# A decoder layer on one core: sums of weights ahead end with job u, u's second column half is requested earlier, the bias is turned two granules sooner

## The chip, the core and the metric

One core of a Trainium2 chip runs the whole kernel as one program. The metric is the device time in microseconds; the kernel before took 1565.01 us (median of 3 runs, 1563.86 to 1565.57). The engines named here are TensorE (PE for its matmuls, PEld for its weight loads), VectorE (DVE), ScalarE (ACT), GpSimd (POOL) and SyncE (SP). SyncE here only issues DMAs (queue q1 in the profile); GpSimd issues the other DMAs (queue q0) beside some elementwise work. Each engine works through its own queue in the order in which the program was written, and waits for the others by semaphores.

## The reference

One layer of a decoder with two mixers side by side, on 512 tokens of width 2048, float32. Cut to what matters:

```python
h = rms_norm(x, norm_g)
proj = h @ w_in                                   # 2048 x 10800
q, kv, g_logits, z_a, uv, z_b, merge_logits = split(proj)
o_a = nsa_attention(q, kv..., g_logits) * silu(z_a)
uv = gelu(uv); u, v = split(uv)                   # 1024 columns each
v = layer_norm(v, ln_v_g, ln_v_b)
o_b = u * (tril(w_s) @ v + b_s) * silu(z_b)       # per group and chunk of 128 tokens
g_a, g_b = split(sigmoid(merge_logits))
x = x + (g_a * (o_a @ w_up_a) + g_b * (o_b @ w_up_b)) @ w_out
x = x + sigmoid(x @ w_ple_gate) * (p @ w_ple)
out = rms_norm(x, final_g)
```

The bias of the title is `b_s` (`sgu_b` in the kernel), 8 groups by 128 positions; `w_s` is `sgu_w`.

## The kernel before

**Products in two parts.** A float32 product is made of three matmuls on rounded parts: each operand is split into a high part (a ScalarE cast, line 142) and a low part (the rest, a VectorE subtraction, line 148), and high x high, low x high and high x low are summed in PSUM (lines 348 to 350).

**Jobs.** All matrix products are jobs in one list, and one generator, `gemm`, issues their matmuls in order. `fill(n)` draws n pieces from it, `finish(name)` draws until a job is done; code between such calls puts its own instructions (transposes, loads, stores) into the stream at that place. The order of everything is thus written out by hand.

**Jobs of kind "S".** They compute 512 tokens by 1024 columns over 2048 rows with seven half-size products instead of eight (Strassen's scheme). The weights fall into four blocks: b11 and b12 (upper rows, first and second half of the columns) and b21 and b22 (lower rows). Products are named 1 to 7. Product 5 uses b12 - b11, 6 uses b22 - that sum, 7 uses the result less b11 (written over b11), 4 uses b21 less what stands in b12 by then. These sums of weights are made on VectorE, in place (`sum_to`, line 255).

**Granules.** A product goes over four pairs of 128-row tiles; such a pair is a granule (an entry of `subs`): 12 matmuls, four draws of `fill`. A job of kind S has 28 granules. Job u (the first half of uv) has the order 1, 2, 5, 6 and 3 in turn, 7, 4; the jobs after it (vn, zb and m0 to m3) run 1 and 5 in turn, 6 and 3, 7, and 2 and 4. Three PSUM banks hold products: 1, 6, 7 and 4 go to the first, 5 and 3 to the second, 2 to the third. So product 4 adds into the banks that product 7 filled, once the additions of line 688 have read them. Products 1, 5 and 6 are first copied out by ScalarE (line 675).

**Loads.** `add_job` lists the weight loads of a job, 512 KB each, in the order in which SyncE issues them. Each tag has a ring of tiles: raw 3 (b21 and b22 pass through it), b11 4, b12 4. `load_next` (line 231) issues loads in that order and stops at the first whose tile isn't free yet, or whose pool isn't open (b12 lives in the pool "quad", which is opened at line 1357, after the attention phase, and lies on memory that the attention's tiles had; line 1361 calls `load_next` right after). For u the order is four b11, four b21, four b12, four b22, and four b21 again (b21').

**Running ahead.** Before the matmuls of granule si, `split_to(si + 2)` issues the high and low parts for granules up to two ahead, the sums for one more, and, where `state["sums"]` is over 1, the sums up to `state["sums"]` granules further. `state["sums"]` is 4 from the end of job za7 to the end of u, and 1 otherwise. `sum_to` leaves off where a load that it needs hasn't been issued, but it doesn't ask whether the load has landed: the VectorE instruction waits for that in its queue.

**Around u.** While u runs, the program loads the bias and the spatial weights (`bn`, `wn`, lines 1366 to 1368), turns them on TensorE in between (lines 1483 to 1495: the bias after 20 draws, the two halves of `wn` after four more each) and then starts the background list: four `oa_chunk`s of 16 items that split the attention output and form its sums (lines 1379 to 1418), drawn `state["pops"]` at a time per granule during u and vn; `assert not background` stands behind vn. The second copy of product 1 (`keep1`) takes the tile that `bn` had (tag "s1", two buffers).

Of the kernel before, what the change touches and what calls it, by code (L numbers as in the profile page):

```python
# [22 lines left out]
S = 512  # L23
# [33 lines left out]
def products(job):  # L57
    return [(p, j) for pair in job.order for j in range(job.kt // 4) for p in pair]
# [6 lines left out]
def kernel(ctx: ExitStack, tc: tile.TileContext, x, p, norm_g, w_in,  # L65
# [15 lines left out]
    def bank(kind, name):  # L81
        return psum.tile([P, 512], F32, tag=kind, name=name)
# [51 lines left out]
    def flush():  # L134
        todo = list(deferred)
        deferred.clear()
        for f in todo:
            f()

    def high(hi, src, scale=None):  # L140
        if scale is None:
            nc.scalar.copy(hi, src)  # L142
        else:
            nc.scalar.mul(hi, src, scale)

    def low(hi, lo, src, scale=None):
        if scale is None:
            nc.vector.tensor_tensor(out=lo, in0=src, in1=hi.bitcast(F32), op=ALU.subtract)  # L148
        else:
            nc.vector.scalar_tensor_tensor(out=lo, in0=src, scalar=scale, in1=hi.bitcast(F32),  # L150
                                           op0=ALU.mult, op1=ALU.subtract)
# [10 lines left out]
    jobs, subs, loads = [], [], []  # L162
# [6 lines left out]
    def add_load(tag, src, n, cols):  # L169
        r = ring_loads[tag]  # L170
        before.append(r[-rings[tag]] if len(r) >= rings[tag] else None)
        r.append(len(loads))
        loads.append((tag, src, n, cols))
        last_sub.append(None)
        return len(loads) - 1

    def weights(job, k, n, c0):
        return job.w[k * P:(k + n) * P, c0:c0 + job.cols].rearrange("(k p) c -> p k c", p=P)

    def add_job(job):  # L180
        jobs.append(job)
        if job.kind == "S":
            half, c2 = job.kt // 2, job.c2
            ld = {}
            direct = job.order[0] == "1"
            for tags in ("b11", "b21", "b12", "b22", "b21'") if direct else (("b11", "b12"), ("b22",), ("b21",)):
                for j in range(half // 2):
                    for tag in (tags,) if direct else tags:
                        c, k = (job.c0, c2)[tag[2] == "2"], half * (tag[1] == "2") + 2 * j
                        ld[tag, j] = add_load(tag if tag[1] == "1" else "raw", weights(job, k, 2, c), 2, job.cols)  # L190
            for p, j in products(job):
                if not direct:
                    ld["b21'", j] = ld["b21", j]
                last = {"7": ("b11",), "4": ("b12", "b21'"), "3": ("b22",)}.get(p, ())
                if direct and p == "2":
                    last = ("b21",)
                for tag in last:
                    last_sub[ld[tag, j]] = len(subs)
                subs.append((job, p, j, ld))
            return  # L200
        first = 0
        while first < job.kt:
            n = min(job.per_load, job.kt - first)
            li = add_load("raw", weights(job, first, n, job.c0), n, job.cols)
            for k in range(first, first + n, job.per_sub):
                last_sub[li] = len(subs)
                subs.append((job, k, min(job.per_sub, first + n - k), (li, first)))
            first += n

    raw, parts = {}, {}  # L210
    state = {"loads": 0, "sum": 0, "high": 0, "low": 0, "ahead": 0, "more": 1, "pops": 2, "due": 0, "b11": 0, "sums": 1}

    def ring(i, dtype, n=2):

# [16 lines left out]
    def load_next():  # L231
        while state["loads"] < len(loads):
            b = before[state["loads"]]
            if b is not None and last_sub[b] >= state["low"]:
                return
            if loads[state["loads"]][0] != "raw" and ("free" if loads[state["loads"]][0] == "b11" else "pool") not in quad:
                return
            load_to(state["loads"])
# [3 lines left out]
    def sum_to(i):  # L242

        while state["sum"] <= min(i, len(subs) - 1):
            job, p, j, ld = subs[state["sum"]]
            if job.kind != "S" or p not in "5674":
                state["sum"] += 1
                continue
            if any(ld[tag, j] not in raw for tag in ("b11", "b12") + {"6": ("b22",), "4": ("b21'",)}.get(p, ())):
                return  # L250
            state["sum"] += 1
            b = {tag: raw[ld[tag, j]] for tag in ("b11", "b12") + {"6": ("b22",), "4": ("b21'",)}.get(p, ())}
            o, x, y = {"5": ("b12", "b12", "b11"), "6": ("b12", "b22", "b12"),
                       "7": ("b11", "b12", "b11"), "4": ("b12", "b21'", "b12")}[p]
            nc.vector.tensor_tensor(out=b[o], in0=b[x], in1=b[y], op=ALU.subtract)  # L255

    def source(i):
        job, k, n, ld = subs[i]
        if job.kind == "S":
            return raw[ld[{"1": "b11", "5": "b12", "6": "b12", "3": "b22", "7": "b11", "2": "b21", "4": "b12"}[k], n]]  # L260
        return raw[ld[0]][:, k - ld[1]:k - ld[1] + n]

    def narrow(job, p):

        return job.kind == "S" and job.order[0] == "1" == p

    def split_to(i, more=1):
        while state["high"] < len(subs):
            h = state["high"]
            job, k, n, ld = subs[h]  # L270
            if h > (i if job.kind == "S" else i + more):
                break
            sum_to(h)
            if job.kind == "S" and narrow(job, k):
                hi = [stream.tile([P, job.cols], F32R, tag="hi", name="hi", bufs=4) for _ in range(2)]
                src = source(h)
                for a in range(2):
                    high(hi[a], src[:, a])
                parts[h] = [hi, None, src]
                state["high"] += 1  # L280
                continue
            if job.kind == "S":
                hi = quad["pool"].tile([P, 2, job.cols], F32R, tag="hs", name="hs", bufs=3)
            elif k >= job.kt - job.tail:
                hi = f_tiles["tail"]("h", k - job.kt + job.tail)
            else:
                hi = stream.tile([P, n, job.cols], F32R, tag="hi", name="hi", bufs=4)
            src = source(h)
            high(hi, src)
            parts[h] = [hi, None, src]  # L290
            state["high"] += 1
        sum_to(i + 1)
        while state["low"] <= min(i, state["high"] - 1):
            job, k, n, ld = subs[state["low"]]
            pt = parts[state["low"]]
            if job.kind == "S" and narrow(job, k):
                pt[1] = [stream.tile([P, job.cols], F32R, tag="lo", name="lo") for _ in range(2)]
                for a in range(2):
                    low(pt[0][a], pt[1][a], pt[2][:, a])
                state["low"] += 1  # L300
                load_next()
                continue
            if job.kind == "S":
                pt[1] = quad["pool"].tile([P, 2, job.cols], F32R, tag="ls", name="ls", bufs=3)
            elif k >= job.kt - job.tail:
                pt[1] = f_tiles["tail"]("l", k - job.kt + job.tail)
            else:
                pt[1] = stream.tile([P, n, job.cols], F32R, tag="lo", name="lo")
            low(*pt)
            state["low"] += 1  # L310
            load_next()
        if state["sums"] > 1:
            sum_to(i + state["sums"])

    done = set()

# [101 lines left out]
    def fill(n):  # L418
        for _ in range(n):
            next(run, None)  # L420

    def finish(name):
        while name not in done:
            next(run)
        flush()
# [192 lines left out]
    for cg in range(4):  # L618
        job = Job(f"pl{cg}", "N", w_ple, 512 * cg, 512, 2, lambda k: (pl_in["h"][:, k], pl_in["l"][:, k]),
                  evac_ple(cg), (xs, ys)[cg % 2])  # L620
        if cg == 0:
            job.per_load = 1
        add_job(job)
# [409 lines left out]
    with tc.tile_pool(name="cmp", bufs=1) as cmp:  # L1033
# [47 lines left out]
        c = cmp.tile([P, 1], F32, name="hid_c")  # L1081
# [235 lines left out]
    for s in range(n + 3):  # L1317
# [4 lines left out]
        if s < n:  # L1322
            ft, j = slots[s][0], s % 6
# [139 lines left out]
    def s4_chunk(c, new_sum=new_sum):  # L1463
# [8 lines left out]
        def second():  # L1472
# [5 lines left out]
    nc.gpsimd.memset(tri, 1.0)  # L1478
    nc.gpsimd.affine_select(out=tri, in_=tri, pattern=[[1, P]], compare_op=ALU.is_ge, fill=0.0,
                            base=0, channel_multiplier=-1)  # L1480
    state["pops"] = 1.33
    state["sums"] = 4
    fill(20)
    b = bank("o", "ps_b")
    nc.tensor.transpose(b[:, :8], bn, ident[:8, :8])
    nc.vector.tensor_copy(sgu_bt, b[:, :8])
# [14 lines left out]
            for i, a in enumerate((act_h, act_l)):  # L1501
                nc.gpsimd.dma_start(a(slice(4 * q, 4 * q + 4), slice(256, 512)), s3_dram[:, i, 4 * q:4 * q + 4])

    finish("u")
    state["sums"] = 1
    finish("vn")
    assert not background

# [358 lines left out]
```

## Time and profile before

| | us |
|---|---|
| median of 3 runs | 1565.01 |
| the profiled execution, its time | 1565.86 |
| its span in the trace | 1564.2 |
| job u, first matmul to that of vn | 489.93 to 580.40 |

The profile is one execution on the chip, times in microseconds from the span's start. A row of the timeline gives start, duration, engine, line of the kernel, operation, the tile written and the tile read, their shapes, how often, and in square brackets the idle time just before it and what ended it. A row of the waits gives who waited for whom, the total, how often and the longest. A row of a window gives its length, the busy time of PE, PEld, DVE, ACT and POOL with the number of instructions, the granted TensorE clock (1.00 is full), the share of the DMA engines and GB/s. A row of DMA issues ends in the KB of each and the median time from issue to landing; a row of a DMA queue gives packets, MB and its share of the 16 engines. Weight tiles read "raw" or "b" (buffer numbers are left out, so b11 and b12 are both "b"); "hs" and "ls" are the high and low parts of a granule.

### The profile page before, as it was taken

How to read it: one execution, taken by the hardware profiler on the slowest of the kernel's cores; microseconds unless marked ns; L12 is line 12 of the kernel's file. 1: busy time of each engine (PE TensorE's matmuls, PEld its weight loads, DVE VectorE, ACT ScalarE, POOL GpSimd, SP SyncE). 2: the span in 40 equal slices, each digit the busy share in tenths (PEclk: the TensorE clock that was granted, in tenths of full speed). 3: DMA queues.
4: the chain of work that ended last, by engine and by line, in shares of the span. 5: the costliest groups of instructions: out<-in, count | busy, mean ns of one | idle time of the engine just before them, and what ended most of it. 6: DMA issues, size and time to landing. Idle time of an engine off the chain costs nothing.

```text
span 1564.2 us, 20523 instructions
## 1 busy us (share of the span) xinstructions
PE 1541.0 (99%) x7438; PEld 1289.5 (82%) x7438; DVE 1194.1 (76%) x1869; ACT 786.0 (50%) x1345; POOL 252.3 (16%) x413
## 2 busy tenths in 40 slices
PE   9999999999999989999999999999999999999997
PEld 7889988888887868888888888888888888888885
DVE  6557758888886877978887777777656587888876
ACT  6434446667665445555544444444423343544555
POOL 1201101101122232301121211220122221000000
PEclk9999999999999999999999999999999999999999
DMA  8436731213235884917473737675742387464665
GB/s 318 129 81 194 221 81 48 61 48 108 74 90 189 245 270 131 287 54 242 133 266 103 270 100 243 206 265 205 265 153 88 122 259 245 148 202 165 185 205 185
DMA packets 161429, 269.23 MB, mean 172 GB/s; under 512 B 9752, under 2 KB 80048, under 8 KB 158768
## 3 DMA queue, kind: packets, MB, share of 16 engines
q1 hardware_dynamic: 116240, 151.67, 31.1%
q0 software_dynamic: 44944, 116.00, 22.3%
q8 instruction: 58, 0.95, 0.2%
q14 instruction: 43, 0.35, 0.1%
q10 hardware_dynamic: 144, 0.26, 0.0%
HBM read 209.69 MB, written 58.20 MB: 171 GB/s over the span
## 4 chain that ended last, share of the span: by engine, by line
PE 93%; DVE 3%; DMA 1%; ACT 1%; issue 1%; DVEq 0%; POOL 0%; SPq 0%; POOLq 0%; ACTq 0%
PE ps_m L348 7%; PE ps_m L349 7%; PE ps_m L350 6%; PE ps_za L374 2%; PE ps_t L1197 2%; PE ps_za L375 2%; PE ps_za L376 2%; PE ps_ub L388 2%; PE ps_wo L386 2%; PE ps_ub L386 2%; PE ps_ub L387 2%; PE ps_wo L387 2%; PE ps_wo L388 2%; PE ps_wo L348 2%; PE ps_pg L348 2%; PE ps_ua L348 2%
## 5 line engine op out<-in xcount | busy, mean ns | idle before, releaser
L148 DVE TENSOR_TENSOR ls<-b,hs 128x1024 fp32r<-128x1024 f32 x196 | 239.7, 1224 | 118.3 <-ACT hs L142 117.3
L142 ACT CAST hs<-b 128x1024 fp32r<-128x1024 f32 x196 | 206.1, 1053 | 236.3 <-PE ps_m L350 86.3
L148 DVE TENSOR_TENSOR lo<-raw,hi 128x512 fp32r<-128x512 f32 (+1 forms) x216 | 151.5, 706 | 80.8 <-issue 24.4
L142 ACT CAST hi<-raw 128x512 fp32r<-128x512 f32 (+1 forms) x216 | 129.3, 606 | 136.2 <-PE ps_ub L388 48.5
L142 ACT CAST hs<-raw 128x1024 fp32r<-128x1024 f32 x80 | 84.1, 1054 | 94.4 <-PE ps_m L350 35.4
L148 DVE TENSOR_TENSOR ls<-raw,hs 128x1024 fp32r<-128x1024 f32 x80 | 97.8, 1222 | 14.0 <-ACT hs L142 13.9
L255 DVE TENSOR_TENSOR b<-b,b 128x1024 f32<-128x1024 f32 x80 | 97.5, 1219 | 10.1 <-DMA b<-in_w_in_dram 10.1
L255 DVE TENSOR_TENSOR b<-raw,b 128x1024 f32<-128x1024 f32 x80 | 97.5, 1219 | 5.2 <-DMA raw<-in_w_in_dram 5.2
L348 PE MATMUL ps_m<-hs,act_h 128*128 128x512 f32 x256 | 100.5, 393 | 0.0
L349 PE MATMUL ps_m<-ls,act_h 128*128 128x512 f32 x256 | 99.7, 389 | 0.0
L350 PE MATMUL ps_m<-hs,act_l 128*128 128x512 f32 x256 | 99.7, 389 | 0.0
L142 ACT CAST pth<-ps_t 128x512 fp32r<-128x512 f32 (+1 forms) x88 | 48.0, 545 | 65.6 <-PE ps_t L1197 65.3
L1158 ACT ACTIVATE prob<-prob,st 128x512 f32<-128x512 f32 (+3 forms) x128 | 70.7, 556 | 4.0 <-DVE st L1149 3.8
L148 DVE TENSOR_TENSOR ptl<-ps_t,pth 128x512 fp32r<-128x512 f32 (+1 forms) x88 | 56.3, 640 | 20.9 <-ACT pth L142 19.9
L1149 DVE CUSTOM_DVE_ANT_0 prob<-ps_s,b 128x512 f32<-128x512 f32 (+3 forms) x128 | 56.3, 486 | 9.9 <-PE ps_s L1146 9.7
L350 PEld LDWEIGHTS ps_m<-hs,act_l 128*128 128x128 f32 x256 | 48.1, 188 | 10.1
L348 PEld LDWEIGHTS ps_m<-hs,act_h 128*128 128x128 f32 x256 | 48.1, 188 | 9.8
L349 PEld LDWEIGHTS ps_m<-ls,act_h 128*128 128x128 f32 x256 | 48.1, 188 | 9.6
L374 PE MATMUL ps_za<-act_h,hi 128*128 128x512 f32 x128 | 55.7, 435 | 0.0
L374 PE MATMUL ps_q<-act_h,hi 128*128 128x512 f32 x128 | 53.6, 419 | 0.0
L1197 PEld LDWEIGHTS ps_t<-ident,prob 128*128 128x128 f32 x320 | 39.7, 140 | 13.7 <-DVE ptl L148 2.8
L1197 PE MATMUL ps_t<-ident,prob 128*128 128x128 f32 x320 | 49.5, 273 | 1.4 <-DVE ptl L148 1.3
(641 smaller groups left out, 4399.5 us busy)
## 6 DMA issues: line engine op xcount, KB each, us to landing
raw<-in_w_in_dram SPq DMA_DIRECT2D x112, 512.0 KB, 3.8
b<-in_w_in_dram SPq DMA_DIRECT2D x56, 512.0 KB, 5.7
raw<-in_w_out_dram SPq DMA_DIRECT2D x24, 512.0 KB, 4.2
raw<-in_w_ple_gate_dram SPq DMA_DIRECT2D x24, 512.0 KB, 4.1
raw<-in_w_up_b_dram SPq DMA_DIRECT2D x16, 512.0 KB, 3.7
hsum<-h_stage POOLq DMA_DIRECT2D x12, 512.0 KB, 4.3
gate<-keep POOLq DMA_DIRECT2D x24, 256.0 KB, 4.5
oa_d<-oa_g POOLq DMA_DIRECT2D x40, 128.0 KB, 3.2
```

Source lines behind the costliest of these rows:

```text
L142: nc.scalar.copy(hi, src)
L148: nc.vector.tensor_tensor(out=lo, in0=src, in1=hi.bitcast(F32), op=ALU.subtract)
L255: nc.vector.tensor_tensor(out=b[o], in0=b[x], in1=b[y], op=ALU.subtract)
L348: nc.tensor.matmul(o, ah, wh, start=st, stop=False, skip_group_check=go)
L349: nc.tensor.matmul(o, ah, wl, start=False, stop=False, skip_group_check=go)
L350: nc.tensor.matmul(o, al, wh, start=False, stop=sp, skip_group_check=go)
L374: nc.tensor.matmul(ps, hi[:, j], ah, start=st, stop=False)
L386: nc.tensor.matmul(o, ah[:, sl], hi[:, j], start=st, stop=False)
L387: nc.tensor.matmul(o, ah[:, sl], lo[:, j], start=False, stop=False)
L388: nc.tensor.matmul(o, al[:, sl], hi[:, j], start=False, stop=sp)
L1158: nc.scalar.activation(sl, sl, AF.Exp, bias=st[:, 0, j, hh:hh + 1], scale=-1.0, accum_out=st[:, 1, j, hh:hh + 1])
L1197: nc.tensor.transpose(b[:, (2 * e + hh) * P:(2 * e + hh + 1) * P], pts[hh][:, c:c + P], ident)
```

## The change

Four edits. First, in u's list of loads the fourth b21 load moves behind the four b12 loads. Second, the extra lookahead of the sums is no longer a state that is set and reset around u: in u it still reaches four granules beyond the granule being split, but not beyond u's last one. Third, the bias is turned after 12 draws instead of 20, three granules into u instead of five, and all that follows it in the program (the turns of `wn`, the start of the background) comes two granules sooner. Fourth, the background is drawn at 1.3 instead of 1.33 items a granule. The call `finish("u")` that stood only to reset the state goes with it.

```diff
@@ add_job
-            for tags in ("b11", "b21", "b12", "b22", "b21'") if direct else (("b11", "b12"), ("b22",), ("b21",)):
-                for j in range(half // 2):
-                    for tag in (tags,) if direct else tags:
-                        c, k = (job.c0, c2)[tag[2] == "2"], half * (tag[1] == "2") + 2 * j
-                        ld[tag, j] = add_load(tag if tag[1] == "1" else "raw", weights(job, k, 2, c), 2, job.cols)
+            groups = [[(tag, j) for j in range(half // 2) for tag in tags] for tags in
+                      ((("b11",), ("b21",), ("b12",), ("b22",), ("b21'",)) if direct else (("b11", "b12"), ("b22",), ("b21",)))]
+            if direct:
+                groups[2].append(groups[1].pop())
+            for group in groups:
+                for tag, j in group:
+                    c, k = (job.c0, c2)[tag[2] == "2"], half * (tag[1] == "2") + 2 * j
+                    ld[tag, j] = add_load(tag if tag[1] == "1" else "raw", weights(job, k, 2, c), 2, job.cols)
@@ split_to, at its end
-        if state["sums"] > 1:
-            sum_to(i + state["sums"])
+        job = subs[min(i, len(subs) - 1)][0]
+        if job.kind == "S" and job.order[0] == "1":
+            more = i + 1
+            while more < i + 4 and subs[more + 1][0] is job:
+                more += 1
+            sum_to(more)
@@ around u
-    state["pops"] = 1.33
-    state["sums"] = 4
-    fill(20)
+    state["pops"] = 1.3
+    fill(12)
     b = bank("o", "ps_b")
     nc.tensor.transpose(b[:, :8], bn, ident[:8, :8])
     nc.vector.tensor_copy(sgu_bt, b[:, :8])
...
-    finish("u")
-    state["sums"] = 1
     finish("vn")
```

More of the change, by code (lines that the diff above doesn't have):

```diff
@@ L210 @@
     raw, parts = {}, {}
-    state = {"loads": 0, "sum": 0, "high": 0, "low": 0, "ahead": 0, "more": 1, "pops": 2, "due": 0, "b11": 0, "sums": 1}
+    state = {"loads": 0, "sum": 0, "high": 0, "low": 0, "ahead": 0, "more": 1, "pops": 2, "due": 0, "b11": 0}
     def ring(i, dtype, n=2):
```

## Prediction

> **What bounds the kernel.** The page of the profile comes first, then the waits of TensorE alone, then the timeline of TensorE, VectorE and the DMA queues where those waits lie.
>
> ```profile
> PE 1541.0 (99%) x7438; PEld 1289.5 (82%) x7438; DVE 1194.1 (76%) x1869; ACT 786.0 (50%) x1345; POOL 252.3 (16%) x413
> ```
>
> ```profile
> PE ps_u L348 <- DVE keep L688: 6.5, 1, 6.5
> PE ps_u L349 <- DVE ls L148: 2.2, 1, 2.2
> ...
> PE ps_t L1197 <- DVE ptl L148: 1.3, 1, 1.3
> ```
>
> TensorE is busy 99% of the span, so only what keeps it waiting, or keeps its clock down, can be won. Two waits of the whole execution are over 2 us, and both lie in job u, the job that is edited. Its matmuls, in the timeline (start, duration):
>
> ```profile
> 489.93 0.39 PE L348 MATMUL ps_u<-hi,act_h 128*128 128x512 f32 x1
> 500.81 0.39 PE L348 MATMUL ps_u<-hs,act_h 128*128 128x512 f32 x1
> 503.62 0.23 PE L1485 MATMUL ps_b<-ident,bn 8*128 8x8 f32 x1
> 503.78 0.49 PE L348 MATMUL ps_u<-hs,act_h 128*128 128x512 f32 x1
> 506.44 0.58 PE L349 MATMUL ps_u<-ls,act_h 128*128 128x512 f32 x1 [2.17 <-DVE ls L148]
> 510.44 0.39 PE L350 MATMUL ps_u<-hs,act_l 128*128 128x512 f32 x1
> 560.56 0.39 PE L350 MATMUL ps_u<-hs,act_l 128*128 128x512 f32 x1
> 567.46 0.76 PE L348 MATMUL ps_u<-hs,act_h 128*128 128x512 f32 x1 [6.52 <-DVE keep L688]
> 571.98 0.40 PE L350 MATMUL ps_u<-hs,act_l 128*128 128x512 f32 x1
> 580.40 0.39 PE L348 MATMUL ps_vn<-hs,act_h 128*128 128x512 f32 x1
> ```
>
> Granules are counted from 0, so u has 0 to 27; each is 12 matmuls. The first four (48 matmuls) run from 489.93 to 500.81: 0.2267 us each, 2.72 us a granule. From 503.78 to 510.44 lie 11 matmuls, 2.49 us at that pace and 6.66 in fact: **4.17 us lost**. From 560.56 to 571.98 lie 12, 2.72 us at that pace and 11.42 in fact: **8.70 us lost**. Together 12.87. As a cross-check, u's 336 matmuls need 76.17 us of the 90.47 between its first and vn's; beside the 12.87 that leaves 1.43 for the nine small transposes in between and a few tenths.
>
> (The matmul at 560.56 is the last of product 7, granule 23.) Part of each loss is idle time, part is clock. The stretch behind the 1.3 us wait of the third line (it ends at 304.3), and the one behind the 2.2 us wait (columns: length, busy us of PE, PEld, DVE, ACT, POOL, granted clock, DMA share, GB/s):
>
> ```profile
> 305.00:308.00 3.00, 3.00 (x19) 2.60 (x19) 2.93 (x14) 2.74 (x10) 0.00 (x0) 1.00 0.00 0
> ```
>
> ```profile
> 506.44:510.20 3.76, 3.76 (x10) 2.97 (x11) 3.76 (x5) 0.01 (x1) 0.00 (x0) 0.55 0.98 335
> ```
>
> After 2.17 us of idle the clock was granted at 0.55 for 3.8 us; after 1.3 us it stayed at 1.00. So a wait of a little over a microsecond costs itself, one of 2.2 costs nearly double. Now what VectorE and the SyncE queue did:
>
> ```profile
> 497.37 1.22 DVE L148 TENSOR_TENSOR ls<-raw,hs 128x1024 fp32r<-128x1024 f32 x1
> 504.03 1.23 DVE L255 TENSOR_TENSOR b<-b,b 128x1024 f32<-128x1024 f32 x1 [5.44 <-DMA b<-in_w_in_dram]
> 505.17 1.22 DVE L148 TENSOR_TENSOR ls<-raw,hs 128x1024 fp32r<-128x1024 f32 x1
> ```
>
> and at the second place:
>
> ```profile
> 559.64 1.22 DVE L148 TENSOR_TENSOR ls<-b,hs 128x1024 fp32r<-128x1024 f32 x1
> 565.49 1.22 DVE L255 TENSOR_TENSOR b<-b,b 128x1024 f32<-128x1024 f32 x1 [4.62 <-DMA b<-in_w_in_dram]
> 566.63 1.28 DVE L688 TENSOR_TENSOR keep<-ps_u,keep 128x512 f32<-128x512 f32 x2
> ```
>
> ```profile
> 498.61 0.37 SPq L227 DMA_DIRECT2D raw<-in_w_in_dram  x1
> 499.09 2.93 SPq L227 DMA_DIRECT2D b<-in_w_in_dram  x4
> ```
>
> Both losses are one mechanism. VectorE runs in order; a sum of weights (L255), asked for ahead of need, stands in its queue before its load has landed, and urgent work stands behind it. At 498.6 the sum is product 5's first (b12 of u), and behind it is the low half of granule 5. At 560.9 it is vn's first sum, and behind it are the two L688 additions that empty the banks into which product 4 must accumulate. The loads are late for a reason, too: the four b12 requests stand in the SyncE queue behind the fourth b21 load, which may go only when VectorE has finished with the first one (498.6).
>
> **The change, part by part.**
>
> *Sums end with u.* The limit i+4 no longer crosses into vn, so vn's first sum is not queued at granule 23. Removes the wait at 560.9: 8.70 us. What is late next: the first matmul of granule 24 is due at 560.79 and needs L688 on its bank. L148 of granule 25 ends at 560.86, one L688 is 0.64 of the pair's 1.28, and 567.46 less 566.63+0.64 gives 0.19 for the signal: 561.7, 0.9 us late. With VectorE a little less behind (it then has not lost 2 us at 533 to a load, nor carried the o_a work, below) 0.4. I take **+0.6**, bounds 0 and 1.0; at that size the clock holds, by the row at 305. vn's sum now comes with the ordinary lookahead, at granule 26, two granules and 0.6 us after 560.79, i.e. 566.8. Its load:
>
> ```profile
> 558.63 6.74 DMA b<-in_w_in_dram
> ```
>
> This is the chain's piece for it: landed at 565.37, ahead of 566.8 (both by the old clock, on which they shift together); cost nothing, its cover is the three granules that the sum goes back.
>
> *b12 asked for ahead of the last b21.* The four requests are now emitted when the pool opens, right after the attention phase. That pool lies on the attention's tiles, whose last reader is the first of these lines of GpSimd; the others are the loads of its queue that follow:
>
> ```profile
> 489.02 0.73 POOL L1234 TENSOR_TENSOR o<-o,oc 128x256 f32<-128x256 f32 x1 [5.11 <-DVE o L1233]
> 489.69 0.56 POOL L1315 DMA_DIRECT2D ob_h<-hsum  x1
> 490.24 0.56 POOL L1315 DMA_DIRECT2D ob_l<-hsum  x1
> 490.77 1.55 POOL L1367 DMA_DIRECT2D wn<-in_sgu_w_dram  x2
> 492.27 0.58 POOL L1368 DMA_DIRECT2D bn<-in_sgu_b_dram  x1
> ```
>
> So b12 goes out at about 489.75 instead of 499.09, 9.3 us sooner, and the SyncE queue has nothing else to do between (its next item, the fourth b21, may not go before 498.6 anyway; it then waits behind at most the rest of b12 and is needed at granule 7, about 509.5). The first b12 took 4.9 us before; even at twice that it lands at 499.6, and the sum has until the low half of granule 5, due at 503.8 less 2.4 of VectorE work, 501.4. The 4.17 us go.
>
> *Bias two granules sooner.* The transpose of bn moves from behind granule 4 (it stands at 503.62) to behind granule 2, due at 489.93 + 36 x 0.2267 = 498.09; the two turns of wn follow a granule each. The instructions stay the same: cost nothing in themselves. They free something: the second keep copy of product 1 shares bn's buffer and waited for that transpose.
>
> ```profile
> 503.88 0.59 ACT L675 COPY keep<-ps_u 128x512 f32<-128x512 f32 x1 [2.97 <-PE ps_b L1485]
> ```
>
> Those 2.97 us of ScalarE lie under VectorE's 5.44 now; they would become the next wait were the bias left in place, and I count them at 0. But bn must have landed at 498.09. Before, its issue at 492.27 plus this row gave 497.1:
>
> ```profile
> bn<-in_sgu_b_dram POOLq DMA_DIRECT2D x1, 4.0 KB, 4.8
> ```
>
> It stands behind 1.57 MB (two of 512 KB, two of 256) in the GpSimd queue, which now shares the engines with 2.1 MB of b12. Where the two queues compete (1116 to 1120, mean 385 GB/s):
>
> ```profile
> q0 software_dynamic: 264, 1.02, 64.6%
> q1 hardware_dynamic: 263, 0.52, 36.5%
> ```
>
> The GpSimd queue keeps two thirds, about 255 KB/us. Some 1.2 MB of it fall after 493, once both are flowing: 4.7 us instead of about 3.6, so bn lands near 498.2, and with 0.2 for the signal TensorE waits **0.3**. Bounds: 0, and all of b12 ahead of bn, 2.1 MB at 385 = 5.4 us, bn at 502.5: 4.4 idle plus a slow stretch like the one above (4.17 less 2.17, 2.0), 6.4. I stay near the lower end, since the shared row is measured.
>
> The Trainium skill bears on the price of such a wait: "TensorE: Matmul & The Clock Gate", section "Why this matters for your kernels", asks for no idle gaps over about 3 us. By that rule a bias wait of 2 us would cost only itself. This trace disagrees: 2.17 us idle was followed by a granted clock of 0.55. By the rule a 2.2 us wait leaves about 10 us of gain, by the trace about 8.
>
> *Background (o_a) two granules sooner, 1.3 instead of 1.33 a granule.* The same VectorE work, two lines like the first, two like the second and one of half size, 3.4 us, over granules 14 to 18 instead of 16 to 20. VectorE is close to full there, and the third line is the tightest point:
>
> ```profile
> 543.17 0.88 DVE L431 TENSOR_TENSOR oa_f<-oa_f 128x256 f32<-128x256 f32 x2
> 549.30 0.69 DVE L150 SCALAR_TENSOR_TENSOR oa_f<-oa_f,oa_g 128x512 fp32r<-128x512 f32 x1
> ...
> 553.97 1.22 DVE L148 TENSOR_TENSOR ls<-b,hs 128x1024 fp32r<-128x1024 f32 x1
> ```
>
> It ends at 555.19; granule 22 is due at 560.79 - 5.44 = 555.35 and uses it in its second matmul, 0.4 us later. Moving o_a forward relieves that point and loads granules 14 to 17 (four low halves and four sums at 1.14 us each, the distance from 504.03 to 505.17, and o_a: 12.5 us of work in 10.9), 1.6 late against a lookahead of two granules, 5.4 us, less one cast and one low half. Cost 0; up to +1.5 if the cover fails; if anything a gain.
>
> Sum: -4.17 - 8.70 + 0.6 + 0.3 = **-12.0 us**. The profiled span of 1564.2 becomes 1552.2. That execution took 1565.86; the median of the runs is 1565.01, and I take the difference from it: **1553.0**.
>
> **Rivals.** (a) *The bias waits long.* If q0's startup suffers, bn lands around 500.3: 2.2 idle and 2.0 of clock, 3.9 more than counted: 1556.9; at the far bound 1559.1. For it: the slack is nil. Against: the two-thirds share. (b) *b12 doesn't go earlier*, because the pool's opening or a semaphore holds SyncE until about 498: the first loss stays, 12.0 - 4.17 + 0.3: 1556.9. Against: the last reader ends at 489.75, and nothing of the DMA engines' own holds it, which are idle just before (last two columns):
>
> ```profile
> 485.00:490.00 5.00, 5.00 (x28) 4.27 (x27) 1.44 (x3) 1.46 (x4) 0.98 (x2) 1.00 0.00 0
> ```
>
> (c) *The wait moves into vn, and it gets slower.* vn's four b12 loads are released by product 4's low halves. If each lands later than its sum stands in the queue and PE pays a loss like the first (4.17), four of them are 16.7: 1569.7. It decides once a load takes more than about 11 us: 6.74 now, 8.2 to the sum's place at 566.8, and from there two granules less a sum, a cast (1.05, the 2.97 us row's engine) and a low half. With two or three such losses the gain is about used up, 1561 to 1565.5. Against: vn's later sums already run with this short lookahead, and no wait of TensorE in vn is on the list. (d) *Only half a gain*: VectorE's piling up at 14 to 17 costs one wait of 2 us with clock: 1557.0.
>
> **Numbers.** Forecast 0.72 (own range 1551.5 to 1554.8: both new waits at nothing give 1565.01 - 12.87 = 1552.1, less a little for o_a's tight point; both at their likelier upper sizes, 1.0 and 1.5, give 1554.6), (a) 0.11, (b) 0.05, (c) 0.07, (d) 0.05. The range 1551.5 to 1557.2 holds the forecast, (b), (d) and half of (a). No change means within 0.2%, 3.1 us, about what a measurement tells apart. Faster 0.93, all but (c); of (c), same 0.02 where two or three of its losses come, slower 0.05 where all four do.
>
> **What would show it.** No VectorE wait on b<-in_w_in_dram in u; b12 issued by SyncE near 490; u from first matmul to vn's in 78.5 us instead of 90.5; the granted clock at 1.00 throughout u; a wait of 0.3 before ps_b and of 0.6 before product 4's first matmul. Wrong if a wait over 2 us on bn, or on b in vn, appears with a slow stretch behind it.

## The result, and the profile after

| | before | after |
|---|---|---|
| median (7 runs each, side by side), us | 1563.86 (1562.82 to 1565.57) | 1559.38 (1559.0 to 1560.73) |
| the profiled execution, its time | 1565.86 | 1559.0 |
| its span | 1564.2 | 1557.3 |
| u's first matmul to vn's | 90.47 | 82.61 |
| wo's first matmul to pg's (two of the last jobs) | 170.64 | 173.15 |

The changed kernel takes 0.9973 of the time before (95% interval 0.9961 to 0.9985): 4.5 us less, where 12.0 had been forecast. 1559.38 lies above the range of 1551.5 to 1557.2.

The page's line of engines and the waits of TensorE in the changed kernel; line numbers have moved by seven (L688 is now L695, L348 to L350 are L355 to L357).

```profile
PE 1538.7 (99%) x7438; PEld 1288.9 (83%) x7438; DVE 1195.3 (77%) x1869; ACT 785.0 (50%) x1345; POOL 252.8 (16%) x413
```

```profile
PE ps_b L1491 <- DMA bn<-in_sgu_b_dram: 2.8, 1, 2.8
PE ps_wo L394 <- DVE lo L148: 2.2, 1, 2.2
...
PE ps_u L355 <- DVE keep L695: 0.4, 1, 0.4
```

Both waits that headed the list before are gone, the 6.5 down to the hand-over of 0.4. Two others stand in their place: TensorE waits 2.8 us for the bias's load, and 2.2 us in wo, 770 us behind the place of the change (wo is the product with `w_out`, pg the one with `w_ple_gate`). TensorE's timeline around u:

```profile
489.60 0.39 PE L355 MATMUL ps_u<-hi,act_h 128*128 128x512 f32 x1
500.72 0.19 PE L1491 MATMUL ps_b<-ident,bn 8*128 8x8 f32 x1 [2.79 <-DMA bn<-in_sgu_b_dram]
502.39 0.63 PE L355 MATMUL ps_u<-hi,act_h 128*128 128x512 f32 x1
561.21 0.47 PE L355 MATMUL ps_u<-hs,act_h 128*128 128x512 f32 x1 [0.38 <-DVE keep L695]
572.21 0.39 PE L355 MATMUL ps_vn<-hs,act_h 128*128 128x512 f32 x1
```

The bias is turned at 500.72; it was due at 497.93. The matmul at 502.39 takes 0.63 instead of 0.39. The windows of the same trace (length, busy PE, PEld, DVE, ACT, POOL, granted clock, DMA share, GB/s) show why:

```profile
498.88:502.30 3.42, 1.58 (x7) 1.35 (x8) 1.87 (x4) 0.00 (x0) 0.00 (x0) 1.00 1.05 407
502.30:505.71 3.41, 3.41 (x12) 2.65 (x11) 1.09 (x1) 1.10 (x3) 0.00 (x0) 0.50 0.79 248
505.71:509.12 3.41, 3.41 (x19) 2.88 (x18) 2.96 (x3) 1.53 (x4) 1.82 (x4) 1.00 0.47 102
```

3.41 us at half clock behind the wait: 1.7 us of work lost, 4.5 with the idle time. So u is shorter by 4.17 + 8.70 - 0.38 - 4.5 = 8.0 by these terms, and by 7.86 in fact. Of the span's 6.9 us less, 7.86 come from u, 0.33 from its earlier start and 1.2 from the last part behind pg's first matmul (176.2 to 174.9; the other traces have 174.7 to 175.4); wo gives 2.51 back. The profiled execution of before took 2.0 us more than the median, that of after 0.4 less, so the medians differ by less than the spans.

The four b12 requests and the bias's load, in the timelines of SyncE's queue and of GpSimd:

```profile
489.44 2.35 SPq L230 DMA_DIRECT2D b<-in_w_in_dram  x4
```

```profile
491.94 0.58 POOL L1375 DMA_DIRECT2D bn<-in_sgu_b_dram  x1
```

And vn's first sum on VectorE, with no bracket behind it: no wait.

```profile
566.53 1.22 DVE L258 TENSOR_TENSOR b<-b,b 128x1024 f32<-128x1024 f32 x1
```

The bias's load took 8.6 us from issue to landing (4.8 before). What the queues moved up to its landing at 500.58 (packets, MB, share of the 16 engines), in 490 to 493 and in 493 to 500.6 of the changed kernel:

```profile
bn<-in_sgu_b_dram POOLq DMA_DIRECT2D x1, 4.0 KB, 8.6
```

```profile
q1 hardware_dynamic: 222, 0.45, 64.5%
q0 software_dynamic: 40, 0.16, 17.2%
```

```profile
q0 software_dynamic: 517, 1.67, 61.6%
q1 hardware_dynamic: 615, 1.17, 43.3%
```

and of the GpSimd queue in the kernel before, in 490 to 493 and in 493 to 497, when the bias landed (497.05):

```profile
q0 software_dynamic: 99, 0.41, 54.1%
```

```profile
q0 software_dynamic: 458, 1.43, 95.1%
```

Up to 493 GpSimd's queue got 0.16 MB through where it had got 0.41, although the changed kernel issues these loads 0.33 us earlier. SyncE's packets were there first: its b12 requests go out at 489.44, GpSimd's first load at 489.37, but up to 492 only SyncE's queue moves anything (0.28 MB); in the kernel before, GpSimd's had moved 0.21 MB by then. From 493 on, in the changed kernel, GpSimd's moved 1.67 MB in 7.6 us, 220 KB/us, instead of 1.43 MB in 4.05. In the rows above a packet of GpSimd's queue carries 3.2 KB (1.67 MB by 517) and one of SyncE's 1.9 KB (1.17 by 615); in the forecast's row near 1116 it was 3.9 and 2.0 KB at 264 to 263 packets. The two queues seem to share by packets rather than by bytes; that is read off these rows and was not varied.

### The profile page after: what moved, and what is told of

Same layout as the page of the kernel before. It is cut to its first block, busy times and chain, and to the rows that moved or that the text cites. A ratio compares the mean times of both kernels' runs of the same rounds, so it can differ in the third digit from the quotient of the medians.

```text
span 1557.3 us, 20518 instructions
## 1 busy us (share of the span) xinstructions
PE 1538.7 (99%) x7438; PEld 1288.9 (83%) x7438; DVE 1195.3 (77%) x1869; ACT 785.0 (50%) x1345; POOL 252.8 (16%) x413
## 4 chain that ended last, share of the span: by engine, by line
PE 94%; DVE 3%; DMA 1%; ACT 1%; issue 1%; POOL 0%; DVEq 0%; POOLq 0%; ACTq 0%
PE ps_m L355 7%; PE ps_m L357 7%; PE ps_m L356 7%; PE ps_t L1204 2%; PE ps_ub L394 2%; PE ps_ub L393 2%; PE ps_ub L395 2%; PE ps_za L381 2%; PE ps_za L382 2%; PE ps_za L383 2%; PE ps_pg L356 2%; PE ps_wo L355 2%; PE ps_pg L357 2%; PE ps_ua L356 2%; PE ps_ua L355 2%; PE ps_zb L356 2%
## 5 line engine op out<-in xcount | busy, mean ns | idle before, releaser
L355 PE MATMUL ps_m<-hs,act_h 128*128 128x512 f32 x256 | 100.5, 393 | 0.0
L357 PE MATMUL ps_m<-hs,act_l 128*128 128x512 f32 x256 | 99.6, 389 | 0.0
L357 PEld LDWEIGHTS ps_m<-hs,act_l 128*128 128x128 f32 x256 | 48.1, 188 | 10.1
L355 PEld LDWEIGHTS ps_m<-hs,act_h 128*128 128x128 f32 x256 | 48.1, 188 | 9.7
L394 PE MATMUL ps_wo<-lo,act_h 128*128 128x512 f32 x128 | 49.9, 390 | 2.2 <-DVE lo L148 2.2
```

The lines of the kernel that those rows point to most:

```text
L355: nc.tensor.matmul(o, ah, wh, start=st, stop=False, skip_group_check=go)
L357: nc.tensor.matmul(o, al, wh, start=False, stop=sp, skip_group_check=go)
L394: nc.tensor.matmul(o, ah[:, sl], lo[:, j], start=False, stop=False)
```

## The experiments

Every experiment but the last was timed in five rounds (the one with 20 draws and 1.33 items a granule has four runs) beside the kernel before, whose medians were 1564.73 (the first four), 1563.98 (the next four) and 1563.62 (the last two). Medians of different groups can thus differ by a microsecond for no reason in the kernel. The edits are those of the section on the change, first to fourth. "Length of u" is from its first matmul to vn's.

### The kernel before with the second edit alone

```diff
-        if state["sums"] > 1:
-            sum_to(i + state["sums"])
+        job = subs[min(i, len(subs) - 1)][0]
+        if job.kind == "S" and job.order[0] == "1":
+            ...
+            sum_to(more)
```

(`state["sums"]` and its call `finish("u")` go with it.)

> Before, with edit 2 alone: sums of weights end with u; the loads' order, the bias after 20 draws and 1.33 items a granule as before. Theory (the bias wait is the price of the change, all else is as forecast): the wait of VectorE on vn's first b12 goes, the one near 504 stays; u takes 90.5 - 8.3 = 82.2 us from its first matmul to vn's, the time falls by about 8. Rival (the gain is taken back behind u, where the changed kernel shows a new wait of 2.2 us in wo): u 82.2 us too, but the time falls by 5 or less.

1556.23 us (1555.85 to 1557.98), ratio 0.995 (0.9937 to 0.9962). Length of u 82.45. Its waits of TensorE:

```profile
PE ps_u L353 <- DVE ls L148: 2.9, 2, 2.5
...
PE ps_u L352 <- DVE keep L692: 0.9, 1, 0.9
```

8.0 us of u's length go: the wait of 6.5 and its slow clock were the sum of vn's in VectorE's queue, as forecast. The hand-over of 0.9 that is left is the size that the forecast worked out for a VectorE that runs behind (0.9, taken at 0.6). One thing was not expected: the first wait stayed, was longer than before (2.54 against 2.17), and the clock stayed full behind it. Windows of this trace:

```profile
501.55:504.96 3.41, 2.29 (x10) 1.42 (x8) 0.99 (x1) 1.50 (x3) 0.76 (x1) 1.00 1.05 389
504.96:508.38 3.42, 1.99 (x9) 1.64 (x10) 3.42 (x4) 1.06 (x2) 1.32 (x3) 1.00 0.92 313
508.38:511.79 3.41, 3.41 (x19) 2.83 (x18) 3.41 (x5) 1.05 (x1) 0.00 (x0) 1.00 1.07 413
```

Here the idle time (503.85 to 506.39) is divided between two windows, and neither is idle for more than 1.43 us. The last section comes back to it.

### The kernel before with the first edit alone

```diff
+            if direct:
+                groups[2].append(groups[1].pop())
```

> Before, with edit 1 alone: b12 asked for ahead of the last b21; sums still cross into vn, bias after 20 draws. Theory: bn lands near 500.5 as in the changed kernel (the queues share), but its transpose stands at 503.3, so nothing waits; the wait near 504 goes, ScalarE's second keep copy still waits for the transpose and may cost up to 0.5; the wait of 8.7 us at 560 stays. u 86.3 to 86.9 us, the time 3.6 to 4.2 below before. Rival (early b12 loads hurt more than the bias, through hsum, b22 or wn): u 88 us or more.

1559.4 us (1558.03 to 1561.03), ratio 0.9968 (0.9955 to 0.998). Length of u 86.67, 3.8 less, as expected; the median falls by 5.3 where 3.6 to 4.2 were expected, the profiled execution, the slowest of the five, by 3.7. The first wait is gone, the second stands unchanged:

```profile
PE ps_u L351 <- DVE keep L691: 6.5, 1, 6.5
```

The bias landed at 500.49, 3.4 us later than before, with the bias's turn still at its old place (503.36), where nobody waited for it. So the delay comes from the first edit, and only the third lets TensorE meet it.

### The changed kernel with the third and fourth edit undone

```diff
-    state["pops"] = 1.3
-    fill(12)
+    state["pops"] = 1.33
+    fill(20)
```

> The changed kernel with edits 3 and 4 undone: bias after 20 draws, 1.33 items a granule. Theory: no wait on bn, so the changed kernel's 2.8 us of idle and 1.7 us of slow clock go; ScalarE's keep copy waits for the transpose again, up to 0.5 us of TensorE; u 78.0 to 78.8 us against 82.6, the time 4 below the changed kernel's 1559.4, 1555 to 1556. Rival (the ScalarE wait of 3 us takes the place of the bias wait): u 80 to 82 us, 1557 to 1559. Rival (taken back behind u): u 78 us, time 1558 or more.

1552.11 us (1551.82 to 1552.4), ratio 0.992 (0.9907 to 0.9934). Length of u 78.31, and neither a wait for the bias nor one in wo; both are undone with these two edits. That is why the time is 3 us below the 1555 to 1556 expected, which left the wait in wo where it was. In u's length the two first edits add up: 8.02 and 3.80 by themselves, 12.16 together. ScalarE does wait for the bias's turn:

```profile
503.58 0.59 ACT L682 COPY keep<-ps_u 128x512 f32<-128x512 f32 x1 [2.97 <-PE ps_b L1491]
```

Nobody on the path waits for ScalarE there. The third edit frees this copy, and gains nothing by it.

### The changed kernel, bias first in GpSimd's queue

```diff
-    load_sums(slice(6, 8))
     ph_ab.close()
     ...
+    nc.gpsimd.dma_start(bn, sgu_b)
     for hf in range(2):
         nc.gpsimd.dma_start(wn[hf], ...)
-    nc.gpsimd.dma_start(bn, sgu_b)
+    load_sums(slice(6, 8))
```

> The changed kernel with the GpSimd queue reordered: bn first, then wn, then the last hsum loads (ob_h, ob_l), instead of ob_h, ob_l, wn, bn. All transfers and the bias's place (12 draws) are as in the changed kernel. Theory: bn lands before 495 beside b12's start, TensorE waits for nothing at 498; wn lands near 497, ahead of its turns; u 77.8 to 78.4 us, 1555 or a little less. Rival (the whole of DMA traffic is too much at this place, so the wait moves to wn or to b12's sums): a new TensorE wait of over 1 us between 498 and 515, u 80 us or more.

1555.7 us (1554.36 to 1557.69), ratio 0.9946 (0.9932 to 0.9959). Length of u 78.16. The bias's load and the waits over 1.5 us:

```profile
bn<-in_sgu_b_dram POOLq DMA_DIRECT2D x1, 4.0 KB, 3.6
```

```profile
PE ps_wo L394 <- DVE lo L148: 2.0, 1, 2.0
```

The same 4 KB land 3.6 us after their issue (at 493.28) when nothing stands ahead of them, with the same b12 loads beside them, and the whole loss near 498 is gone. It was the queue, not the turn of the bias. The wait in wo stays, so it has another cause.

### The wait in wo: the counter of the background

Each granule adds `state["pops"]` to `state["due"]` and draws one item for every whole unit; the rest is carried on. u, vn and zb are 84 granules: 84 x 1.33 = 111.72 leaves 0.72 in the counter, 84 x 1.3 = 109.2 leaves 0.20. Behind zb the rate is set anew, the counter is not. This kernel is the changed one with the old remainder put in:

```diff
     for g in range(8):
         background.extend(group(g))
-    state["pops"] = 1
+    state["pops"], state["due"] = 1, 0.72
```

> The changed kernel with one number put back: behind job zb the fraction of a background item that is carried on (state due) is set to 0.72, what 84 granules at 1.33 leave, instead of 0.20, what 84 at 1.3 leave. u, vn and zb are untouched. Theory (the carried fraction shifts the sums of wo by a granule, and that makes the new wait of 2.2 us near 1273): u 82.6 us as in the changed kernel, with its wait on bn; no wait of TensorE over 1 us in wo; the time 2.5 to 3.5 below the changed kernel's, 1556 to 1557. Rival (the wait in wo comes from u ending earlier, or by chance): wo keeps a wait of about 2 us, 1559 to 1560.

1554.98 us (1554.64 to 1556.22), ratio 0.9944 (0.9932 to 0.9957): 4.4 us less than the changed kernel by the medians, where 2.5 to 3.5 were expected (the part on why the prediction was wrong comes back to it). Length of u 82.68 with the bias's wait of 2.87 as before; no wait in wo, whose length is 170.62. GpSimd in wo, first in the changed kernel:

```profile
1258.34 0.72 POOL L1459 DMA_DIRECT2D s_d<-stage  x1 [2.82 <-DVE stage L148]
1259.05 0.77 POOL L1678 DMA_DIRECT2D x_d<-x  x1
1261.59 1.38 POOL L1723 DMA_DIRECT2D x2t_d<-x2t  x2 [1.76 <-DVE x2t L148]
```

then in this one:

```profile
1253.93 0.72 POOL L1459 DMA_DIRECT2D s_d<-stage  x1 [1.24 <-DVE stage L148]
1256.32 0.78 POOL L1678 DMA_DIRECT2D x_d<-x  x1 [1.67 <-DVE x L815]
1261.50 1.38 POOL L1723 DMA_DIRECT2D x2t_d<-x2t  x2 [4.40 <-DVE x2t L148]
```

At 0.7 items a granule the smaller remainder puts a background sum one granule later. Its store (s_d) comes 4.4 us later, and the store of x (x_d, 1 MB), which stands behind it in GpSimd's queue, 2.7 us. The two x2t stores (512 KB each) are issued at the same time in both kernels, but in the changed one behind an x_d that is still under way. Its row there, issue to landing:

```profile
x_d<-x POOLq DMA_DIRECT2D x1, 1024.0 KB, 7.3
```

and with the old remainder, where it has landed at 1260.9:

```profile
x_d<-x POOLq DMA_DIRECT2D x1, 1024.0 KB, 4.6
```

The landing of the x2t stores releases a tile for which ScalarE waits, in the changed kernel and then in this one:

```profile
1270.70 0.59 ACT L142 CAST x2t<-ps_x 128x512 fp32r<-128x512 f32 x1 [6.33 <-DMA x2t_d<-x2t]
```

```profile
1266.20 1.07 ACT L142 CAST x2t<-ps_x 128x512 fp32r<-128x512 f32 x2 [1.87 <-DMA x2t_d<-x2t]
```

VectorE's half of the same split waits for ScalarE (the row names its next copy, line 1698), and wo's next low part stands behind it in VectorE's queue (the changed kernel):

```profile
1272.60 1.29 DVE L148 TENSOR_TENSOR x2t<-ps_x,x2t 128x512 fp32r<-128x512 f32 x2 [5.11 <-ACT third L1698]
1273.80 0.74 DVE L438 TENSOR_TENSOR third<-ps_x,third 128x256 f32<-128x256 f32 x2
1274.46 0.68 DVE L148 TENSOR_TENSOR lo<-raw,hi 128x512 fp32r<-128x512 f32 x1
```

TensorE waits for that low part until 1275.20. All twelve traces divide the same way: where the remainder is 0.20, ScalarE waits 6.1 to 6.4 us there, where it is 0.72, 1.7 to 2.6. In kind it is the loss of before again: work that may wait stands in VectorE's queue ahead of work that may not.

The cross-check puts the new remainder into the kernel with 20 draws and 1.33 a granule, which had no wait in wo:

```diff
-    state["pops"] = 1
+    state["pops"], state["due"] = 1, 0.2
```

> The kernel with the bias after 20 draws and 1.33 items a granule (the two other edits in), with the carried fraction set to 0.20 behind zb. Theory: u as there, 78.3 us; the wait of about 2 us in wo appears, 1555 to 1556 against 1552.1 without it. Rival (by chance, or by u's length): no wait in wo, 1552.

1553.82 us (1553.54 to 1554.44), ratio 0.9935 (0.9923 to 0.9948): 1.7 us more than with 0.72, and 2.5 more when each is set against the before beside it; 1555 to 1556 had been expected. The wait comes back with nothing else changed:

```profile
PE ps_wo L394 <- DVE lo L148: 1.7, 1, 1.7
```

### The changed kernel with the first edit undone

```diff
-            if direct:
-                groups[2].append(groups[1].pop())
```

> The changed kernel with edit 1 alone undone: b12 again behind the fourth b21; sums end with u, bias after 12 draws, 1.3 items. Theory (bn is late because b12 shares the DMA engines with the GpSimd queue): bn lands near 497.0, TensorE doesn't wait for it at 498; the wait of VectorE on b12 near 504 is back, about 4 us of TensorE; u 81.5 to 82.5 us; with the wait in wo 1558.5 to 1560. Rival (bn is late by its place in GpSimd's queue or the transpose costs more there): a wait of over 1.5 us before the bias's transpose, u 84 us or more.

1558.7 us (1556.25 to 1559.21), ratio 0.9963 (0.9951 to 0.9975), not to be told from the 0.9973 of the changed kernel. The bias landed at 496.72 and nobody waited for it. Length of u 80.53, about a microsecond shorter than expected. VectorE waits for b12 as before (until 503.97), but the late b12 costs TensorE waits of 1.2 and 0.2 only, and no half-clock window.

```profile
PE ps_wo L391 <- DVE lo L148: 2.0, 1, 2.0
...
PE ps_w L1494 <- DVE small L1489: 1.2, 1, 1.2
```

So in the changed kernel, beside an early turn of the bias, the first edit trades these 1.4 us for a wait of 2.8 and its half-clock window, and by the medians it is worth nothing there, though it is worth 3.8 us of u's length where the bias stays.

### Both causes mended

Bias first in GpSimd's queue, and 0.72 in the counter (the two diffs above together).

> The kernel with bn ahead in GpSimd's queue (12 draws, 1.3 items), with the carried fraction put back to 0.72. Theory: u 78.2 us, no wait of over 1 us behind it, 1552 against 1555.7 with the fraction at 0.20. Rival: 1555 to 1556.

1551.96 us (1551.76 to 1553.47), ratio 0.9925 (0.9911 to 0.9938). Length of u 78.14. That is 12.0 us less than the 1563.98 of before beside it, the forecast's gain (the rival, 1555 to 1556, is out). With both causes taken away nothing of the shortfall is left.

### Bias after 16 draws

```diff
-    state["pops"] = 1.3
-    fill(12)
+    state["pops"] = 1.33
+    fill(16)
```

> The changed kernel with 16 background items in the first fill of place 0 of u's first group (12 in the change, 20 before) and 1.33 items a granule (1.3 in the change). The bias's row landed at 500.5 us wherever four b12 loads went out ahead of it and the three small loads kept their order. Theory (the bias's turn waits for its load, and its cost is its place): four draws of the first part's items set off the transpose of the bias about 1.4 us later each two granules per eight draws, so near 500.5 us, and TensorE waits 0 to 1 us there, without a stretch at half clock; the carried fraction is 0.72, so no wait in wo. Length of u 78.2 to 79.5 us, time about 1552 to 1553 us against 1564 before. Rival (any wait at the bias is followed by the stretch at half clock): length of u 80 us or more, time near 1555 us.

1551.7 us (1551.37 to 1552.73), ratio 0.9923 (0.9909 to 0.9936). Length of u 78.23. (In the expectation the step is misstated: four draws are one granule, 2.72 us.)

```profile
500.03 0.22 PE L1491 MATMUL ps_b<-ident,bn 8*128 8x8 f32 x1
```

One granule later the place and the load meet, and nothing is waited for. The three kernels without either wait, this one, the last and the one with 20 draws, lie within 0.4 us of each other: where the bias stands matters only as long as it doesn't come ahead of its load.

### The changed kernel once more

> The changed kernel once more, for a second profile of it. Theory: the wait for the bias (2.8 us near 498 us) and the wait in wo (2.2 us near 1273 us) come again at the same places within 0.3 us, since both come from the program's order; whether the stretch of 3.4 us at half clock follows either of them may differ from execution to execution, and that makes up the spread of this kernel's times. Rival: the stretch behind the bias's wait always comes and the one in wo never does, so that the two profiles agree within 0.5 us.

One execution, 1559.84 us, span 1558.1. Both waits came at their places:

```profile
PE ps_b L1491 <- DMA bn<-in_sgu_b_dram: 2.7, 1, 2.7
PE ps_wo L394 <- DVE lo L148: 2.1, 1, 2.1
```

but the clock went down already during the wait for the bias, and for two windows:

```profile
496.23:499.65 3.42, 1.43 (x7) 0.85 (x5) 2.90 (x3) 1.27 (x2) 0.00 (x0) 1.00 1.04 401
499.65:503.06 3.41, 2.66 (x7) 2.18 (x8) 2.38 (x3) 0.00 (x0) 0.00 (x0) 0.50 0.96 367
503.06:506.47 3.41, 3.41 (x11) 2.63 (x10) 0.06 (x1) 0.96 (x2) 0.00 (x0) 0.50 0.50 157
```

6.1 us of matmuls at half clock cost 3.0, so this time the bias's wait cost 5.8 where it cost 4.5 in the first profile, and u is 83.76 long. Half of the rival came true: in both profiles of this kernel a half-clock window follows the bias's wait and none follows the one in wo. But the two executions are 0.84 us apart and not within 0.5, since the first kind came once in one and twice in the other.

## Why the prediction was wrong

**Right: the mechanism and both gains.** VectorE's wait on a weight load is gone from both places, b12 goes out at 489.4 (forecast "about 489.75"), vn's first sum starts at 566.53 (forecast 566.8) without a wait, vn itself is as long as before (76.16), and the hand-over from product 7 to product 4 costs 0.38 where 0.6 was forecast with 0.4 as the lower reading. The background work two granules sooner makes no wait at granules 14 to 17. Rivals (b), (c) and (d) didn't come. With the two causes below mended, the measured gain is the forecast's 12.0; the three kernels without the two waits have u 78.1 to 78.3 long, against 78.5. To the tenth that is luck: u alone is 12.2 to 12.3 us shorter there, since the waits counted at 0.6 and 0.3 came at 0.4 to 0.5 and 0.

**Wrong, first: the term "TensorE waits 0.3" for the bias.** The place was right (due at 498.09 by the forecast, 497.93 in fact). The step that failed is "some 1.2 MB of it fall after 493 ... bn lands near 498.2". From the rows of the queues: in the kernel before 1.43 MB, not 1.2, passed between 493 and the bias's landing; at the assumed 255 KB/us they take 5.6 us, landing 498.6 (0.4 more). The queue got 0.25 MB less through before 493 than in the kernel before: 1.0. It then ran at 220 KB/us, not 255: 7.6 us for 1.67 MB instead of 6.55, another 1.0. Together 500.6, as measured. The reading of the shared rate was near (q0 had 59% of the bytes, two thirds were taken); what it was applied to was not: in the row at 1116 both queues had long been flowing, here the other was at the engines first. Rival (a), whose condition was "if q0's startup suffers", is what happened; its 500.3 and its 2.2 + 2.0 us were nearly right (500.58; 2.8 + 1.7 in one profile, 2.7 + 3.0 in the other). The chance of 0.11 for it was too low for a slack of nil. The forecast's own sign of being wrong, a wait over 2 us on bn with a slow stretch behind it, is what came. The price of 2.0 for the slow stretch had been read from one wait; the last section shows that the price isn't fixed by the wait's length.

**Wrong, second: "1.3 instead of 1.33 a granule ... cost 0".** Its cover was looked for in u alone, and there it is indeed free. The rate also sets what is left in the counter behind zb, 0.20 instead of 0.72, and that moves the background of a job that runs 770 us later by one granule. It costs 2.5, 2.3 and 2.0 us of wo's length in the profiles (changed kernel, bias first, 20 draws, each with and without). By the medians, each set against the before beside it, it costs 4.5, 3.0 and 2.5. No rival had it.

**Together.** The medians give 1559.38 for the changed kernel and 1551.96 with both mended, 7.4 us. The waits alone are 2.8 and 2.2. A half-clock window behind the bias's wait is in all three profiles with that wait, 1.7 to 3.0 us; with it, and the few tenths by which wo is lengthened beyond its wait, the two causes make 7.0 of the 7.4 in the profile of the changed kernel. A window behind the wait in wo is in one of five profiles (the changed kernel with the first edit undone). That such windows come in some executions only is likely the reason why the medians put the wait in wo at more than wo's length: with the old remainder, two of the five runs have 1556.2 us at a granted clock of 0.997, one of them the profiled one with a half-clock window in u, and three have 1554.6 to 1555.0 at 0.998. No trace of the latter was kept, so this share is not shown.

**Base.** The forecast was laid on the median of three runs, 1565.01; in the runs beside the experiments the kernel before had 1563.6 to 1564.7. That is why a gain of 12.0 ends at 1552.0 and not at 1553.0. Next to the two errors it is small.

## What to carry to other kernels

A transfer that is moved ahead takes its bandwidth from whatever was being loaded there: look for the small load at the end of the other queue whose user stands at a fixed place, and either put it first in its queue or leave its user where it was. A rate with a carried remainder is state for everything that comes behind: after a change to it, compare the remainder at each later change of rate, or set it there. When two edits bring the gain and others only follow along, test them apart; here the two that followed gave back about 7.4 of 12.0 us, and the first two alone with the bias where it stood beat the whole change.

## What the hardware showed that was not expected

Idle times of nearly equal length had different prices: 2.17 us (before, near 504) was followed by 3.41 us at half clock, 2.54 (the second edit alone) and 2.2 (wo, changed kernel) by none, 2.75 by 6.8. In every trace the changes of the granted clock lie whole multiples of 3.413 us apart (499.65, 506.47 and 1550.95 in the last run: 2 and 306 times), on a grid whose phase differs from one execution to the next. Laid out on that grid, the price is decided by how much of one window is idle. The wait in wo falls on either side of the limit in two kernels. With 20 draws and 0.2 in the counter the clock stays:

```profile
1268.16:1271.57 3.41, 1.79 (x8) 1.49 (x9) 3.38 (x7) 1.10 (x2) 2.84 (x4) 1.00 0.76 238
1271.57:1274.98 3.41, 3.41 (x17) 2.83 (x16) 3.38 (x7) 2.42 (x5) 0.00 (x0) 1.00 0.96 230
```

In the changed kernel with the first edit undone it goes down:

```profile
1270.93:1274.35 3.42, 1.55 (x7) 1.29 (x8) 3.42 (x7) 1.69 (x4) 2.85 (x4) 1.00 0.67 213
1274.35:1277.76 3.41, 3.41 (x10) 2.67 (x9) 3.34 (x7) 1.76 (x3) 0.30 (x1) 0.50 1.01 231
```

In all nine traces with such waits, a window at full clock with at most 1.58 us busy (498.88 of the changed kernel) is followed by one at half clock, one with at least 1.79 is not: in these traces the limit lies between, about half a window. In these traces a window at half clock is followed by full clock only if it was busy throughout (503.06 above); 2.66 busy (499.65) was not enough. The Trainium skill's page "TensorE: Matmul & The Clock Gate", section "What's actually happening", has the free-running window of 3413 ns, and the traces agree. The same page's table of states asks for a whole idle window before the clock goes down, and here 1.84 us of idle in a window were enough. So by this limit a wait under about 1.6 us costs itself, and a longer one costs more in those executions in which too much of it falls into one window: 1.7 us (one half-clock window, 2.79 of wait in the changed kernel) or 3.0 (two, the last run), and nothing in others (2.54, the second edit alone). The spread of the kernel with the bias first (1554.36 to 1557.69) may come from there, but not all spread does: the three kernels without either wait spread over 0.6, 1.4 and 1.7 us. No run was made that varies the phase on purpose.
